# Batched products of x and y: output tiles of four heads, stored in 32 KB runs

## The chip, the core and the metric

The kernel runs on one core of a Trainium2 chip. The metric is the device time of one execution in microseconds (us), and lower is better. The core has five engines: TensorE (PE, matrix products), VectorE (DVE), ScalarE (ACT), GpSimd (POOL) and SyncE (SP, which here issues transfers), and 16 DMA engines that move data between the chip's main memory (HBM) and the on-chip memory (SBUF, 128 partitions). PE writes its products to PSUM, 128 partitions of eight banks of 2 KB. Weight loads of PE have a row of their own, PEld.

## The reference

```
x: (8, 12, 512, 64) float32      y: (8, 12, 512, 64) float32
out = np.einsum('bhtc,bhsc->bhts', x, y)      # (8, 12, 512, 512) float32
```

For each of the 96 heads (8 batches of 12) the output is the 512 x 512 matrix of dot products of the rows of x with the rows of y, over 64 channels. The inputs are 25.17 MB together, the output is 100.66 MB.

## The kernel before

The heads are taken in six groups of 16. One load brings x or y of a group, 2 MB, as 128 partitions of 64 rows of 64 channels (16 KB each), so that eight partitions hold a head. There are 12 loads, x and y in turn, numbered n = 0 to 11.

Each group is worked on in two halves of eight heads (turns; 12 in all). Several steps turn a loaded tile into operands of PE:

- `compress(n)`: x is cast to bf16 by ACT into `xk`. y is cast in four pieces of 64 partitions into `yb`, two for each half; DVE makes two, POOL and ACT one each (`in_front`).
- `mix(i, name, part)`: four copies of 32 partitions place x of half i in `xb`, in every second bf16 word; the other words stay zero from a memset, so that a product over 128 rows picks out one of two heads' rows. POOL makes these copies for halves 0 to 2, DVE for the rest.
- `transposes(i)`: DVE transposes `xb` into `xT` and `yb` into `yT`, in 32 x 32 blocks. There are two each of `xb`, `xT` and `yT`, one for each parity of the turn.
- `products()`: PE's whole program, a loop with waits. For each of four values of h (a pair of heads) it multiplies eight times 128 columns of `xT` with 512 of `yT`. Four matmuls fill a PSUM tile `pm` of four banks; there are two such tiles, and together they are all of PSUM. PE waits on the semaphore `turned` for a turn's operands and on `taken` for a free `pm`.
- `result(o, s)`: ACT copies the two `pm` tiles of output tile o into the slot s (L251), and `store` sends the slot out. An output tile is 128 partitions of 8 rows of 512 floats: 16 KB in each partition, and 16 KB in one run in HBM.

Loads and output tiles share five slots of 16 KB per partition, dealt out in turn by `slot()`. Each slot has a semaphore of its own for its transfers. Stores are issued by SP, but by ACT for every third tile and the last four:

```
    def by_act(o):
        return o % 3 == 2 or o >= V * NH - V
```

The order on each engine is the order of the Python program; `emit` works out the waits from what each step reads and writes. The last block lays the front out by hand: five loads, two memsets, then for each n the cast, one mixing copy on POOL, the next load, and from n = 8 on the first results among the casts. After it, each turn i is four results, then `prepare(i + 2)`: the transposes for turn i + 2 and DVE's four mixing copies for turn i + 3.

Of the kernel before, what the change touches and what calls it, by code (L numbers as in the profile page):

```python
# [10 lines left out]
def kernel(  # L11
# [25 lines left out]
    P = 128  # L37
# [6 lines left out]
    K = 8  # L44
    E = R // K
    D = 32
    SLOTS = 5
# [9 lines left out]
        "(o u h q n) -> o h q u n", u=2, h=V, q=Q * E, n=K * S  # L57
# [7 lines left out]
    xbs = [sb.tile([P, K * E * D], u32, name=f"xb{half}") for half in range(2)]  # L65
    xTs = [sb.tile([P, K * D * E], u32, name=f"xT{i}") for i in range(2)]
    yTs = [sb.tile([P, D * R // 2], u32, name=f"yT{i}") for i in range(2)]
# [10 lines left out]
    def need(name, points):  # L78

        best = {}  # L80
        for p, v in points:
            if known[name].get(p, 0) < v:
                best[p] = max(best.get(p, 0), v)
        for p, v in list(best.items()):
            if any(snaps[q, w].get(p, 0) >= v for q, w in best.items() if q != p):
                del best[p]
        if name == "pe":
            asked.append(best)
        for p, v in best.items():
            if name != "pe":  # L90
                engines[name].wait_ge(sems[p], v)  # L91
            known[name][p] = v
            for q, w in snaps[p, v].items():
                known[name][q] = max(known[name].get(q, 0), w)

    def emit(name, make, reads=(), writes=(), dma=None, tells=None):

        points = [writer[r] for r in (*reads, *writes) if r in writer]
        points += [v for w in writes for v in readers.get(w, ())]
        if name == "pool" and name in ticks:  # L100
            points.append((name, ticks[name]))
        need(name, points)
        p, step = (tells or name, 1) if dma is None else (f"dma{dma}", 16)
        sem(p)
        at = (p, ticks.get(p, 0) + step)
        ticks[p] = at[1]
        snaps[at] = {**known[name], p: at[1]}
        if dma is None:
            own[name][p] = at[1]
            snaps[at].update(own[name])  # L110
        if name != "pe":
            make().then_inc(sems[p], step)
        for r in reads:
            readers.setdefault(r, []).append(at)
        for w in writes:
            writer[w], readers[w] = at, []

    made_slots, loaded, later, asked = [], {}, [], []
    in_front = ["dve", "pool", "dve", "act"]

    def copy(name, dst, src, reads, writes, tells=None):
        emit(
            name,
            lambda: nc.scalar.activation(dst, src, COPY)  # L124
            if name == "act"
            else engines[name].tensor_copy(dst, src),  # L126
            reads,
            writes,
            tells=tells,
        )  # L130

    def both(i):
        return [("slot", i, 0), ("slot", i, 1)]

    def slot():
        made_slots.append(len(made_slots) % SLOTS)
        return made_slots[-1]

    def load(n):
        i = loaded[n] = slot()  # L140
        emit(
            "sp",
            lambda: nc.sync.dma_start(slots[i], (yv if n % 2 else xv)[n // 2]),  # L143
            writes=both(i),
            dma=i,
        )

    def compress(n):

        i = loaded.pop(n)  # L150
        g = n // 2
        if n % 2 == 0:
            xk = g % (NG - 1)
            dst = xks[xk].rearrange("p r c -> p (r c)")
            copy("act", dst, slots[i], both(i), [("xk", xk)])
            return
        ys = slots[i].rearrange("p (r c) -> p r c", c=C)
        for half in range(2):
            b = g % (NG - 1 + half)
            yv2 = ybs[half][b].bitcast(bf16).rearrange("p (j c w) -> p j w c", j=R // 2, w=2)  # L160
            for ch in range(2):
                copy(
                    in_front[2 * half + ch],
                    yv2[ch * 64:(ch + 1) * 64],
                    ys[half * 64:(half + 1) * 64, :, ch * D:(ch + 1) * D].rearrange(
                        "p (j w) c -> p j w c", w=2
                    ),
                    both(i),
                    [("yb", half, b, ch)],
                )  # L170

    def mix(i, name, part):
# [5 lines left out]
        xv2 = xbs[half].bitcast(bf16).rearrange("p (k e c u) -> p k e c u", k=K, e=E, u=2)  # L178
        copy(
            name,  # L180
            xv2[part * D:(part + 1) * D, :, :, :, u],
            xks[xk][lo:lo + D, :, ch * D:(ch + 1) * D].rearrange("p (e k) c -> p k e c", k=K),
            [("xk", xk)],
            [("xb", half, part)],
        )

    def transposes(i):
        g, half = divmod(i, 2)
        b = g % (NG - 1 + half)
        emit(  # L190
            "dve",
            lambda: nc.vector.transpose(  # L192
                xTs[half].rearrange("p (k r e) -> p k e r", k=K, e=E),
                xbs[half].rearrange("p (k e c) -> p k e c", k=K, e=E),
            ),
            [("xb", half, part) for part in range(4)],
            [("xT", half)],
        )
        emit(
            "dve",  # L200
            lambda: nc.vector.transpose(  # L201
                yTs[half].rearrange("p (r j) -> p j r", r=D),
# [3 lines left out]
            [("yT", half)],  # L206
            tells="turned",
        )

    def products():  # L210

        pe = mybir.EngineType.PE
        with nc.Fori(0, NH // 2, engines=OrderedEngineSet([pe])) as turn:
            for half in range(2):
                xT = xTs[half].bitcast(bf16).rearrange("p (k h m) -> p k h m", k=K, h=V)
                yT = yTs[half].bitcast(bf16)
                nc.tensor.wait_ge(sem("turned"), turn * 2 + (half + 1))
                for h in range(V):
                    for k in range(0, K, 4):
                        done = 2 * (half * V + h) + k // 4  # L220
                        nc.tensor.wait_ge(sem("taken"), turn * (4 * V) + (done + 1))
                        for j in range(4):
                            last = nc.tensor.matmul(  # L223
                                pms[k // 4][:, j, :], xT[:, k + j, h, :], yT[:, h * S:(h + 1) * S],
                                start=True, stop=True,
                            )
                        last.then_inc(sem("pe"), 1)

    def by_act(o):
        return o % 3 == 2 or o >= V * NH - V  # L230

    def store(o, s):
        i, h = divmod(o, V)
        name = "act" if by_act(o) else "sp"
        emit(
            name,
            lambda: engines[name].dma_start(ov[i, h], slots[s]),
            reads=both(s),
            dma=s,
        )  # L240

    def result(o, s):

        ot = slots[s].rearrange("p (r s) -> p r s", s=S)
        for k in range(0, K, 4):
            pm = k // 4
            half = o // V % 2
            emit("pe", None, [("xT", half), ("yT", half)], [("pm", pm)])
            want = {"turned": o // V + 1, "taken": 2 * o + pm + 1}
            assert all(want.get(p, 0) >= v for p, v in asked[-1].items()), (o, k, asked[-1])  # L250
            copy("act", ot[:, k:k + 4, :], pms[pm], [("pm", pm)], [("slot", s, pm)], "taken")  # L251
            if k == 0:
                while later:
                    store(*later.pop())
        if by_act(o):
            later.append((o, s))
        else:
            store(o, s)

    def prepare(i):  # L260

        if i < NH:
            transposes(i)
        if i + 1 < NH:
            for part in range(4):
                mix(i + 1, "dve", part)

    with tc.tile_critical():  # L268
        nc.scalar.sem_inc(sem("taken"), 2)
        ticks["taken"] = 2  # L270
        for g in range(SLOTS):
            load(g)
        for half, name in enumerate(("dve", "pool")):
            emit(
                name,
                lambda: engines[name].memset(xbs[half], 0.0),  # L276
                writes=[("xb", half, part) for part in range(4)],
            )
        front = []
        for n in range(2 * NG):  # L280
            if n == 11:
                result(3, slot())
            compress(n)
            mix(n // 4, "pool", n % 4)
            if n == 4:
                transposes(0)
            if n < 5:
                load(n + SLOTS)
            elif n in (6, 8):
                load(n // 2 + 7)  # L290
            elif n < 10:
                front.append(slot())
            if n > 7 and n < 11:
                result(n - 8, front[n - 8])
            if n == 9:
                transposes(1)
        prepare(2)
        for o in range(V, V * NH):
            result(o, slot())
            if o % V == V - 1:  # L300
                prepare(o // V + 2)
        store(*later.pop())
        products()
        for i, name in enumerate(("dve", "pool", "dve", "sp", "act")):
            need(name, [(f"dma{i}", ticks[f"dma{i}"])])
# [30 lines left out]
```

## Time and profile before

| | |
|---|---|
| median of 3 runs | 301.12 us (301.08 to 301.19) |
| the profiled execution: its time, its span | 301.19 us, 299.4 us |
| ACT busy | 211.0 us (70%) |
| DVE busy | 151.8 us (51%) |
| PE busy, mean granted clock | 127.1 us (42%), 0.834 |
| POOL busy | 56.1 us (19%) |
| DMA moved | 125.85 MB, mean 420 GB/s |
| stores issued by SP, by ACT | 30, 18 (2 MB each) |
| loads issued by SP | 12 (2 MB each) |

The span runs from the first to the last instruction of the profiled execution; its time also holds what lies around that. Busy times overlap, since the engines run side by side. A group of instructions is named by line, engine, operation and tiles, output first (`slot<-pm` is a copy out of PSUM). Idle time is put down to what ended it.

### The profile page before, as it was taken

What the parts mean: (1) busy time and instruction counts of PE and PEld (TensorE: products, weight loads), DVE (VectorE), ACT (ScalarE), POOL (GpSimd) and SP (SyncE); (2) the same over time, 40 slices, a digit from 0 to 9 for tenths busy, and PEclk for the clock granted to TensorE, in tenths of its full rate; (3) what the DMA queues carried; (4) which work ended last, traced back from release to release, by engine and by line L of the source; (5) the groups of instructions that cost most, each with busy time, mean ns of one, the idle gap of its engine ahead of it and who ended that gap; (6) DMA issues with size and microseconds to landing.
All of it is one profiled execution on the core that took longest, in us unless ns stands there. A gap on an engine that the chain in (4) does not pass through costs nothing.

```text
span 299.4 us, 1276 instructions
## 1 busy us (share of the span) xinstructions
PE 127.1 (42%) x378; PEld 34.5 (12%) x384; DVE 151.8 (51%) x73; ACT 211.0 (70%) x109; POOL 56.1 (19%) x23
## 2 busy tenths in 40 slices
PE   0000040546566554565544556454646454736000
PEld 0000010111111111111111111111111111111000
DVE  2167897999839592920946729219276340000000
ACT  1665676999999886767686868585959595959400
POOL 2399999991000000000000000000000000000000
PEclk9999999958799979695979595979595979596855
DMA  7999999999999999999999999999999999999995
GB/s 276 423 433 433 427 423 431 431 429 425 427 438 427 431 436 428 429 433 431 429 433 430 425 429 440 425 427 433 427 429 425 425 429 427 429 427 425 429 427 234
DMA packets 8643, 125.85 MB, mean 420 GB/s; under 512 B 961, under 2 KB 961, under 8 KB 961
## 3 DMA queue, kind: packets, MB, share of 16 engines
q1 hardware_dynamic: 6048, 88.08, 69.3%
q10 hardware_dynamic: 2592, 37.75, 29.6%
q14 instruction: 3, 0.02, 0.0%
HBM read 25.17 MB, written 100.66 MB: 420 GB/s over the span
## 4 chain that ended last, share of the span: by engine, by line
DMA 57%; ACT 22%; PE 6%; issue 6%; DVE 2%; SPq 0%; ACTq 0%
DMA out_dram<-slot 44%; ACT slot L124 20%; DMA slot<-in_y_dram 7%; DMA slot<-in_x_dram 6%; PE pm L223 6%; DVE yb L126 2%; ACT xk L124 1%; ACT yb L124 1%; SPq L143 0%; ACTq L91 0%; SPq L331 0%; SPq L268 0%
## 5 line engine op out<-in xcount | busy, mean ns | idle before, releaser
L124 ACT ACTIVATE slot<-pm 128x2048 f32<-128x2048 f32 x96 | 173.4, 1885 | 46.6 <-DMA out_dram<-slot 43.5
L223 PE MATMUL pm<-yT,xT 128*128 128x512 bf16 x378 | 127.1, 473 | 150.5 <-ACT slot L124 112.5
L192 DVE STREAM_TRANSPOSE xT<-xb 128x2048 uint32<-128x2048 uint32 x12 | 46.6, 3885 | 71.4 <-PE pm L223 69.0
L223 PEld LDWEIGHTS pm<-yT,xT 128*128 128x128 bf16 x384 | 34.5, 111 | 242.6 <-ACT slot L124 170.5
L126 DVE COPY xb<-xk 32x2048 bf16<-32x2048 bf16 x36 | 46.9, 1303 | 1.0
L126 DVE CAST yb<-slot 64x2048 bf16<-64x2048 f32 x12 | 36.2, 3019 | 17.0 <-DMA slot<-in_y_dram 16.8
L126 POOL COPY xb<-xk 32x2048 bf16<-32x2048 bf16 x12 | 36.3, 3022 | 10.5 <-ACT xk L124 9.7
L124 ACT ACTIVATE xk<-slot 128x4096 bf16<-128x4096 f32 x6 | 21.7, 3617 | 16.3 <-DMA slot<-in_x_dram 16.3
L201 DVE STREAM_TRANSPOSE yT<-yb 128x1024 uint32<-128x1024 uint32 x12 | 23.1, 1923 | 0.0
L124 ACT ACTIVATE yb<-slot 64x2048 bf16<-64x2048 f32 x6 | 14.8, 2464 | 5.1 <-DMA slot<-in_y_dram 5.1
L126 POOL CAST yb<-slot 64x2048 bf16<-64x2048 f32 x6 | 17.8, 2968 | 1.4 <-DMA slot<-in_y_dram 0.8
L276 DVE MEMSET xb<- 128x2048 uint32 x1 | 1.8, 1765 | 1.4 <-SPq L268 1.4
L124 ACT ACT_TABLE_LOAD x1 | 1.3, 1283 | 1.0 <-SPq L268 1.0
L276 POOL MEMSET xb<- 128x2048 uint32 x1 | 1.8, 1804 | 0.5 <-SPq L268 0.5
L320 POOL MEMSET const-float32-0.0<- 128x1 f32 x1 | 0.1, 97 | 0.2 <-issue 0.2
L320 POOL MEMSET const-float32-1.0<- 128x1 f32 x1 | 0.1, 98 | 0.0
L320 POOL MEMSET const-bfloat16-1.0<- 128x1 bf16 x1 | 0.1, 98 | 0.0
L320 POOL MEMSET const-uint8-127<- 128x1 uint8 x1 | 0.1, 98 | 0.0
## 6 DMA issues: line engine op xcount, KB each, us to landing
out_dram<-slot SPq DMA_DIRECT2D x30, 2048.0 KB, 16.6
out_dram<-slot ACTq DMA_DIRECT2D x18, 2048.0 KB, 14.7
slot<-in_x_dram SPq DMA_DIRECT2D x6, 2048.0 KB, 17.6
slot<-in_y_dram SPq DMA_DIRECT2D x6, 2048.0 KB, 20.8
```

The costliest lines, as they stand in the source:

```text
L124: lambda: nc.scalar.activation(dst, src, COPY)
L126: else engines[name].tensor_copy(dst, src),
L192: lambda: nc.vector.transpose(xTs[half].rearrange("p (k r e) -> p k e r", k=K, e=E), xbs[half].rearrange("p (k e c) -> p k e c", k=K, e=E),),
L201: lambda: nc.vector.transpose(yTs[half].rearrange("p (r j) -> p j r", r=D), ybs[half][b].rearrange("p (j c) -> p j c", c=D),),
L223: last = nc.tensor.matmul(pms[k // 4][:, j, :], xT[:, k + j, h, :], yT[:, h * S:(h + 1) * S], start=True, stop=True,)
L276: lambda: engines[name].memset(xbs[half], 0.0),
L320: nc = _bacc.Bacc("TRN2", target_bir_lowering=False, num_devices=1)
```

## The change

- K, the rows of an output tile in one partition, goes from 8 to 16, and the 64 rows of an input partition are split as 4 x 16 (E = 4). An output tile o now covers four heads: 128 partitions of 32 KB, 4 MB, and there are 24. Each partition's 32 KB are one run in HBM. All stores are issued by SP.
- There are three slots of 32 KB per partition instead of five of 16 KB. A load takes half a slot (`space`), which gives six load places, each with a semaphore of its own; stores have one for each slot. Load n + 6 goes to the place of load n.
- A matmul has 64 columns of `xT` instead of 128, and its product goes to 64 partitions of a bank. Two of them, one for each of two heads and placed at columns 0 and 64 (`tile_position`), fill a bank. A unit of work is four banks with eight matmuls, and ACT copies it as before, 128 x 2048. There are 96 units as before, eight in a turn.
- There is one `xb`, one `yT`, and one pair of `xT` that holds the two halves of K of one turn. `transposes(i)` is now three steps of 1024 words per partition: the first half of x, y, the second half of x. PE waits for two of them before a turn's first unit and for the third before its third.
- The front: six loads, one memset on POOL, then for n = 0 to 5 load n + 6 behind the casts of n. POOL mixes halves 0 and 1 only, and takes two casts of y for n = 9 and 11 and all of x for n = 10, where ACT did them. DVE mixes from half 2 on. The first units come among the casts from n = 7 on.
- PE itself adds the two free `pm` to `taken`, and the final waits for the last three stores stand on PE, SP and ACT.

The diff, cut to what acts:

```diff
     NG = B * H // G
     NH = 2 * NG
     V = G // 4
-    K = 8
+    K = 16
     E = R // K
     D = 32
-    SLOTS = 5
+    U = K // 4
+    SLOTS = 3
...
     ov = out.rearrange("b h t s -> (b h t s)").rearrange(
-        "(o u h q n) -> o h q u n", u=2, h=V, q=Q * E, n=K * S
+        "(o u t q n) -> o t q u n", u=2, t=2, q=2 * Q * E, n=K * S
     )
 
...
-    xbs = [sb.tile([P, K * E * D], u32, name=f"xb{half}") for half in range(2)]
-    xTs = [sb.tile([P, K * D * E], u32, name=f"xT{i}") for i in range(2)]
-    yTs = [sb.tile([P, D * R // 2], u32, name=f"yT{i}") for i in range(2)]
+    xb = sb.tile([P, R * D], u32, name="xb")
+    xTs = [sb.tile([P, K // 2 * D * E], u32, name=f"xT{i}") for i in range(2)]
+    yT = sb.tile([P, D * R // 2], u32, name="yT")
...
+    def caster(n, half, ch):
+        if n % 2 == 0:
+            return "pool" if n == 10 else "act"
+        return ("dve", "pool", "dve", "pool" if n > 8 else "act")[2 * half + ch]
+
...
+    def space(n):
+        i, j = divmod(n % (2 * SLOTS), 2)
+        return slots[i][:, j * (K * S // 2):(j + 1) * (K * S // 2)], [("slot", i, 2 * j), ("slot", i, 2 * j + 1)]
 
     def load(n):
-        i = loaded[n] = slot()
+        to, where = space(n)
         emit(
             "sp",
-            lambda: nc.sync.dma_start(slots[i], (yv if n % 2 else xv)[n // 2]),
-            writes=both(i),
-            dma=i,
+            lambda: nc.sync.dma_start(to, (yv if n % 2 else xv)[n // 2]),
+            writes=where,
+            dma=f"in{n % (2 * SLOTS)}",
         )
 
...
     def transposes(i):
         g, half = divmod(i, 2)
         b = g % (NG - 1 + half)
+        xe = xb.rearrange("p (e k c) -> p e k c", e=E, c=D)
+
+        def of_x(kh):
+            emit(
+                "dve",
+                lambda: nc.vector.transpose(
+                    xTs[kh].rearrange("p (k r e) -> p e k r", r=D, e=E),
+                    xe[:, :, kh * (K // 2):(kh + 1) * (K // 2), :],
+                ),
+                [("xb", part) for part in range(4)],
+                [("xT", kh)],
+                tells="turned",
+            )
+
+        of_x(0)
         emit(
             "dve",
             lambda: nc.vector.transpose(
-                xTs[half].rearrange("p (k r e) -> p k e r", k=K, e=E),
-                xbs[half].rearrange("p (k e c) -> p k e c", k=K, e=E),
-            ),
-            [("xb", half, part) for part in range(4)],
-            [("xT", half)],
-        )
-        emit(
-            "dve",
-            lambda: nc.vector.transpose(
-                yTs[half].rearrange("p (r j) -> p j r", r=D),
+                yT.rearrange("p (r j) -> p j r", r=D),
                 ybs[half][b].rearrange("p (j c) -> p j c", c=D),
             ),
             [("yb", half, b, ch) for ch in range(2)],
-            [("yT", half)],
+            ["yT"],
             tells="turned",
         )
+        of_x(1)
 
     def products():
 
         pe = mybir.EngineType.PE
-        with nc.Fori(0, NH // 2, engines=OrderedEngineSet([pe])) as turn:
-            for half in range(2):
-                xT = xTs[half].bitcast(bf16).rearrange("p (k h m) -> p k h m", k=K, h=V)
-                yT = yTs[half].bitcast(bf16)
-                nc.tensor.wait_ge(sem("turned"), turn * 2 + (half + 1))
-                for h in range(V):
-                    for k in range(0, K, 4):
-                        done = 2 * (half * V + h) + k // 4
-                        nc.tensor.wait_ge(sem("taken"), turn * (4 * V) + (done + 1))
-                        for j in range(4):
+        xcs = [t.bitcast(bf16).rearrange("p (k h m) -> p k h m", k=K // 2, h=V) for t in xTs]
+        yc = yT.bitcast(bf16)
+        nc.tensor.sem_inc(sem("taken"), 2)
+        with nc.Fori(0, NH, engines=OrderedEngineSet([pe])) as turn:
+            for t in range(2):
+                for v in range(U):
+                    done = t * U + v
+                    if done in (0, U // 2):
+                        nc.tensor.wait_ge(sem("turned"), turn * 3 + (2 + (done > 0)))
+                    nc.tensor.wait_ge(sem("taken"), turn * (2 * U) + (done + 1))
+                    for j in range(4):
+                        kh, k = divmod(4 * v + j, K // 2)
+                        for hs in range(2):
+                            h = 2 * t + hs
                             last = nc.tensor.matmul(
-                                pms[k // 4][:, j, :], xT[:, k + j, h, :], yT[:, h * S:(h + 1) * S],
-                                start=True, stop=True,
+                                pms[v % 2][hs * 64:(hs + 1) * 64, j, :], xcs[kh][:, k, h, :], yc[:, h * S:(h + 1) * S],
+                                start=True, stop=True, tile_position=(0, hs * 64),
                             )
-                        last.then_inc(sem("pe"), 1)
-
-    def by_act(o):
-        return o % 3 == 2 or o >= V * NH - V
-
-    def store(o, s):
-        i, h = divmod(o, V)
-        name = "act" if by_act(o) else "sp"
-        emit(
-            name,
-            lambda: engines[name].dma_start(ov[i, h], slots[s]),
-            reads=both(s),
-            dma=s,
-        )
-
-    def result(o, s):
-
-        ot = slots[s].rearrange("p (r s) -> p r s", s=S)
-        for k in range(0, K, 4):
-            pm = k // 4
-            half = o // V % 2
-            emit("pe", None, [("xT", half), ("yT", half)], [("pm", pm)])
-            want = {"turned": o // V + 1, "taken": 2 * o + pm + 1}
-            assert all(want.get(p, 0) >= v for p, v in asked[-1].items()), (o, k, asked[-1])
-            copy("act", ot[:, k:k + 4, :], pms[pm], [("pm", pm)], [("slot", s, pm)], "taken")
-            if k == 0:
-                while later:
-                    store(*later.pop())
-        if by_act(o):
-            later.append((o, s))
-        else:
-            store(o, s)
-
-    def prepare(i):
-
-        if i < NH:
-            transposes(i)
-        if i + 1 < NH:
-            for part in range(4):
-                mix(i + 1, "dve", part)
+                    last.then_inc(sem("pe"), 1)
+
+    def unit(o, v):
+
+        i = o // 2
+        pm = v % 2
+        emit("pe", None, [("xT", v // 2), "yT"], [("pm", pm)], virtual=True)
+        want = {"turned": 3 * i + (2 if o % 2 == 0 and v < 2 else 3), "taken": o * U + v + 1}
+        assert all(want.get(p, 0) >= w for p, w in asked[-1].items()), (o, v, asked[-1])
+        s = o % SLOTS
+        rows = slots[s].rearrange("p (r s) -> p r s", s=S)[:, 4 * v:4 * v + 4, :]
+        copy("act", rows, pms[pm], [("pm", pm)], [("slot", s, v)], "taken")
+        if v == U - 1:
+            emit(
+                "sp",
+                lambda: nc.sync.dma_start(ov[i, o % 2], slots[s]),
+                reads=[("slot", s, w) for w in range(U)],
+                dma=f"out{s}",
+            )
 
     with tc.tile_critical():
-        nc.scalar.sem_inc(sem("taken"), 2)
+        sem("taken")
         ticks["taken"] = 2
-        for g in range(SLOTS):
-            load(g)
-        for half, name in enumerate(("dve", "pool")):
-            emit(
-                name,
-                lambda: engines[name].memset(xbs[half], 0.0),
-                writes=[("xb", half, part) for part in range(4)],
-            )
-        front = []
+        for n in range(2 * SLOTS):
+            load(n)
+        emit("pool", lambda: nc.gpsimd.memset(xb, 0.0), writes=[("xb", part) for part in range(4)])
         for n in range(2 * NG):
-            if n == 11:
-                result(3, slot())
             compress(n)
-            mix(n // 4, "pool", n % 4)
-            if n == 4:
+            if n < 2 * SLOTS:
+                load(n + 2 * SLOTS)
+            if n < 8:
+                mix(n // 4, "pool", n % 4)
+            if n == 3:
                 transposes(0)
-            if n < 5:
-                load(n + SLOTS)
-            elif n in (6, 8):
-                load(n // 2 + 7)
-            elif n < 10:
-                front.append(slot())
-            if n > 7 and n < 11:
-                result(n - 8, front[n - 8])
-            if n == 9:
+            if 6 < n < 11:
+                for v in (0, 1) if n % 2 else (2, 3):
+                    unit((n - 7) // 2, v)
+            if n == 10:
                 transposes(1)
-        prepare(2)
-        for o in range(V, V * NH):
-            result(o, slot())
-            if o % V == V - 1:
-                prepare(o // V + 2)
-        store(*later.pop())
+        for part in range(4):
+            mix(2, "dve", part)
+        for i in range(1, NH):
+            for o in (2 * i, 2 * i + 1):
+                for v in range(U):
+                    unit(o, v)
+            if i + 1 < NH:
+                transposes(i + 1)
+            if i + 2 < NH:
+                for part in range(4):
+                    mix(i + 2, "dve", part)
         products()
-        for i, name in enumerate(("dve", "pool", "dve", "sp", "act")):
-            need(name, [(f"dma{i}", ticks[f"dma{i}"])])
+        for name, o in (("pe", 2 * NH - 3), ("sp", 2 * NH - 2), ("act", 2 * NH - 1)):
+            need(name, [(f"out{o % SLOTS}", ticks[f"out{o % SLOTS}"])])
```

More of the change, by code (lines that the diff above doesn't have):

```diff
@@ L76, in sem, with need @@
         return sems[p]
-    def need(name, points):
+    def need(name, points, virtual=False):
         best = {}
@@ L86, in need @@
                 del best[p]
-        if name == "pe":
+        if virtual:
             asked.append(best)
         for p, v in best.items():
-            if name != "pe":
+            if not virtual:
                 engines[name].wait_ge(sems[p], v)
@@ L94, in need, with emit @@
                 known[name][q] = max(known[name].get(q, 0), w)
-    def emit(name, make, reads=(), writes=(), dma=None, tells=None):
+    def emit(name, make, reads=(), writes=(), dma=None, tells=None, virtual=False):
         points = [writer[r] for r in (*reads, *writes) if r in writer]
@@ L101, in emit @@
             points.append((name, ticks[name]))
-        need(name, points)
-        p, step = (tells or name, 1) if dma is None else (f"dma{dma}", 16)
+        need(name, points, virtual)
+        p, step = (tells or name, 1) if dma is None else (dma, 16)
         sem(p)
@@ L110, in emit @@
             snaps[at].update(own[name])
-        if name != "pe":
+        if not virtual:
             make().then_inc(sems[p], step)
@@ L116, in emit, with copy @@
             writer[w], readers[w] = at, []
-    made_slots, loaded, later, asked = [], {}, [], []
-    in_front = ["dve", "pool", "dve", "act"]
-    def copy(name, dst, src, reads, writes, tells=None):
+    asked = []
+    def caster(n, half, ch):
+        if n % 2 == 0:
+            return "pool" if n == 10 else "act"
+        return ("dve", "pool", "dve", "pool" if n > 8 else "act")[2 * half + ch]
+    def copy(name, dst, src, reads, writes, tells=None, virtual=False):
         emit(
@@ L129, in copy @@
             tells=tells,
+            virtual=virtual,
         )
[L132 to L137, printed above, removed]
+    def space(n):
+        i, j = divmod(n % (2 * SLOTS), 2)
+        return slots[i][:, j * (K * S // 2):(j + 1) * (K * S // 2)], [("slot", i, 2 * j), ("slot", i, 2 * j + 1)]
     def load(n):
-        i = loaded[n] = slot()
+        to, where = space(n)
         emit(
             "sp",
-            lambda: nc.sync.dma_start(slots[i], (yv if n % 2 else xv)[n // 2]),
-            writes=both(i),
-            dma=i,
+            lambda: nc.sync.dma_start(to, (yv if n % 2 else xv)[n // 2]),
+            writes=where,
+            dma=f"in{n % (2 * SLOTS)}",
         )
     def compress(n):
-        i = loaded.pop(n)
         g = n // 2
+        held, where = space(n)
         if n % 2 == 0:
@@ L154, in compress @@
             dst = xks[xk].rearrange("p r c -> p (r c)")
-            copy("act", dst, slots[i], both(i), [("xk", xk)])
+            copy(caster(n, 0, 0), dst, held, where, [("xk", xk)])
             return
-        ys = slots[i].rearrange("p (r c) -> p r c", c=C)
+        ys = held.rearrange("p (r c) -> p r c", c=C)
         for half in range(2):
@@ L162, in compress @@
                 copy(
-                    in_front[2 * half + ch],
+                    caster(n, half, ch),
                     yv2[ch * 64:(ch + 1) * 64],
@@ L167, in compress @@
                     ),
-                    both(i),
+                    where,
                     [("yb", half, b, ch)],
@@ L177, in mix @@
         xk = g % (NG - 1)
-        xv2 = xbs[half].bitcast(bf16).rearrange("p (k e c u) -> p k e c u", k=K, e=E, u=2)
         copy(
             name,
-            xv2[part * D:(part + 1) * D, :, :, :, u],
-            xks[xk][lo:lo + D, :, ch * D:(ch + 1) * D].rearrange("p (e k) c -> p k e c", k=K),
+            xb[part * D:(part + 1) * D].bitcast(bf16).rearrange("p (r c u) -> p r c u", c=D, u=2)[:, :, :, u],
+            xks[xk][lo:lo + D, :, ch * D:(ch + 1) * D],
             [("xk", xk)],
-            [("xb", half, part)],
+            [("xb", part)],
         )
```

## The prediction

> **What bounds the kernel now.** I read the page's DMA rows first, since 125.85 MB must move whatever the engines do. DMA is the mean busy share of 16 DMA engines, in tenths, over 40 slices of the span.
>
> ```profile
> PE 127.1 (42%) x378; PEld 34.5 (12%) x384; DVE 151.8 (51%) x73; ACT 211.0 (70%) x109; POOL 56.1 (19%) x23
> ...
> DMA  7999999999999999999999999999999999999995
> GB/s 276 423 433 433 427 423 431 431 429 425 427 438 427 431 436 428 429 433 431 429 433 430 425 429 440 425 427 433 427 429 425 425 429 427 429 427 425 429 427 234
> DMA packets 8643, 125.85 MB, mean 420 GB/s; under 512 B 961, under 2 KB 961, under 8 KB 961
> ```
>
> Only the first and the last slice are not full, and no engine is above 70%. The timeline (start, duration, engine, work, idle before it) shows loads landing back to back, since each of these waits ends on a landing:
>
> ```profile
> 8.79 3.62 ACT L124 ACTIVATE xk<-slot 128x4096 bf16<-128x4096 f32 x1 [6.54 <-DMA slot<-in_x_dram]
> ...
> 13.66 2.44 ACT L124 ACTIVATE yb<-slot 64x2048 bf16<-64x2048 f32 x1 [1.25 <-DMA slot<-in_y_dram]
> ...
> 18.56 3.62 ACT L124 ACTIVATE xk<-slot 128x4096 bf16<-128x4096 f32 x1 [2.46 <-DMA slot<-in_x_dram]
> ```
>
> One 2 MB transfer takes 4.88 us. Twelve loads and 48 stores are 60 x 4.88 = 292.8 us; 3.9 before the first and 2.7 after the last make the 299.4 span. The profiled execution took 301.19, 1.79 beyond its span; the runs' median is 301.12, 0.07 away. So two things can move the time: the rate of the queue, and a moment at which it runs dry. What could dry it is in the groups (busy us, mean ns of one, idle before and its releaser) and in the timeline of PE:
>
> ```profile
> L124 ACT ACTIVATE slot<-pm 128x2048 f32<-128x2048 f32 x96 | 173.4, 1885 | 46.6 <-DMA out_dram<-slot 43.5
> ...
> L223 PEld LDWEIGHTS pm<-yT,xT 128*128 128x128 bf16 x384 | 34.5, 111 | 242.6 <-ACT slot L124 170.5
> L126 DVE COPY xb<-xk 32x2048 bf16<-32x2048 bf16 x36 | 46.9, 1303 | 1.0
> ...
> L126 POOL COPY xb<-xk 32x2048 bf16<-32x2048 bf16 x12 | 36.3, 3022 | 10.5 <-ACT xk L124 9.7
> ...
> L201 DVE STREAM_TRANSPOSE yT<-yb 128x1024 uint32<-128x1024 uint32 x12 | 23.1, 1923 | 0.0
> ...
> L126 POOL CAST yb<-slot 64x2048 bf16<-64x2048 f32 x6 | 17.8, 2968 | 1.4 <-DMA slot<-in_y_dram 0.8
> ```
> ```profile
> 176.84 1.04 PE L223 MATMUL pm<-yT,xT 128*128 128x512 bf16 x4 [0.73 <-ACT slot L124]
> ...
> 182.34 3.66 PE L223 MATMUL pm<-yT,xT 128*128 128x512 bf16 x8 [4.46 <-ACT slot L124]
> ```
>
> ACT's copies idle 43.5 us for stores to land: the engines are ahead of the queue. Four matmuls take 1.04 us at the full granted clock and half of 3.66, 1.83 us, after a pause.
>
> **Stores of 32 KB runs.** The 24 stores of 4 MB replace 48 of 2 MB: the same bytes, half as many runs. In the trace's packet records a 16 KB run takes a median 611 ns of its DMA engine, and the only other size, two 8 KB instruction fetches during the run, 309. A line through both is 302 ns per 8 KB and 7 ns fixed, so 32 KB should take 1215 instead of 1222. Each engine moves 24 x 8 = 192 such runs: 192 x 7 = 1.3 us. Each store ends with a 9 ns semaphore packet per engine; 24 fewer are 0.2 us. Sum: -1.5 us, all on the path. Bounds: the best 16 KB packet took 608 ns, the mean 615, so 384 packets at the best are -2.8; stores after 200 us ran at 616, and all 384 at that instead of the mean 614 of the store phase are +0.8. No gain at all if runs are cut at 16 KB, the largest packet shown. I take -1.5, the line through the two sizes.
>
> The Trainium skill (DMA: Bandwidth & Descriptors, Anatomy of one DMA) fits a fixed 2.0 us per DMA plus bytes over 436 GB/s; 24 fewer DMAs would then save 48 us. The trace speaks against charging that here: 4.88 us from landing to landing is 0.07 above 2 MB at the page's 436 GB/s, so back-to-back transfers hide the fixed part.
>
> All stores now go out by SP; before, 18 went by ACT. One queue alone held 430 GB/s from 10 to 50 us, as fast as two later, so this costs nothing. SP has two 0.54 us issues per turn of 8 units, far apart.
>
> **Columns in halves.** A unit (4 PSUM banks, one 1.885 us copy) was 4 matmuls and is now 8 of 64 columns, two per bank. The trace has no such matmul. If the two halves run side by side, a unit stays at 1.04 to 1.83 us; if one after the other, at 2.08 to 3.66. I take side by side: the nearest row fills the same 128 columns from the same 128 rows. A unit may take up to 2.2 us before it matters (below).
>
> The skill speaks against it (TensorEngine Tiling (Array Packing), Gotcha 2): column tiling excludes Fast Weight Load. By the trace a weight load is 111 ns and lies beside running matmuls; eight laid bare would be 0.9 us per unit, 1.9 us at the full clock, still under the limit, and 2.7 on the slow one, over it.
>
> **One set of transposed inputs.** yT and the second half of xT of turn i+1 wait until PE has done turn i. Then DVE turns yT (1.92), PE fills a unit (1.83) while ACT still copies the last one (1.885): ACT idles some 1.9 us once per turn. A turn is 8 x 1.885 + 1.9 = 17.0 us of ACT; its two stores take 2 x 9.77 = 19.5. DVE spends 3 x 1.92 + 4 x 1.30 = 11.0 per turn. Both stay under the queue: zero, with 2.5 us per turn of cover. If PE sets the pace instead, 8 units + 2 us pass 19.5 when a unit passes 2.2.
>
> **Three slots.** A slot lands, is filled in 7.5 us (9.5 across a turn), is issued, and its first packet follows about 1.0 us later (load 0: issued at 0.96, first packet at 1.98). The other two slots cover 2 x 9.77 = 19.5 us. Zero; 9 us of cover.
>
> **The front.** Six loads start at once instead of five; the seventh is issued when ACT has cast x0 (12.4) and the twelfth after y2's casts (about 44), before its turn at 57.7. Loads end at 62.6 as now. With one xb, POOL's mixing of part 4 waits until DVE has transposed all of half 0: the fourth part is ready at 31.3 as now, three transposes end at 37.1. From there POOL has 4 mixes, 6 casts of y and all of x5 (two casts' worth, 5.9): 4 x 3.02 + 6 x 2.97 + 5.9 = 35.8, done at 72.9. DVE, with casts of 3.4 us beside POOL and transposes of half 1 until 67, ends y5 at about 74. ACT: x3 to 41.8, y3 to 45.5, two units to 49.3, x4 to 52.9, two more to 56.7, where store 0 is issued, 6 us before the loads end. Stores 0 and 1 keep the queue busy to 82.1. Store 2 needs y5's place: 74 + 2 x 1.885 = 77.8, and it must be issued 1.5 us before 82.1, so by 80.6. Zero, with 2.8 us of cover, the thinnest here. With POOL at its slowest rows (3.45, 3.54, 7.1) it ends at 79.2 and store 2 is 2.4 us late. Later stores gain 2.5 us per turn.
>
> **Sum.** 301.2 - 1.5 = 299.7 us, span 297.9. The old tail stays, as the last store still ends in a landing.
>
> **Rivals.** (1) The long run is no cheaper (cut at 16 KB, or at the late rows' rate): 301.0, from 300.9 to 302.0. For it: nothing above 16 KB is shown. Against: the 8 and 16 KB rows. (2) Store 2 late, by up to 2.4 us: 299.7 to 302.1, with no gain on the runs up to 303.5; it decides once y5's place is free later than 76.8. For it: POOL takes on x5 and idles to 37.1. Against: its mean rows. (3) Slower: on PE, the halves of a bank follow one another. It decides at 2.2 us per unit. At the mean clock of 0.81 the x4 row becomes 2 x 1.04 / 0.81 = 2.57, a turn 22.5, 3.0 more than the queue needs, over 11 turns +33: 333 us. For it: the row's pauses and the 1.83 us. Against: at the full clock 2.08 fits, and the granted clock was 1.00 from 90 to 100 us, when units came every 1.77 us.
>
> **How the numbers follow.** What a measurement of this kernel can tell from no change is about 0.2%, 0.6 us. My forecast, 0.56: faster. Rival 1, 0.16 (0.14 same, 0.02 slower); rival 2, 0.15 (faster 0.02, same 0.04, slower 0.09); rival 3, 0.13 (slower). So faster 0.58, same 0.18, slower 0.24. The range runs from 298.4 (every packet at the best, -2.8) to 303.0, near the end of rival 2; rival 3 and little else is left out.
>
> **What would show it.** Right: half the store packets, at 1212 to 1216 ns; ACT's group still idle on out_dram; two-store spacing of 19.4; DMA full in every inner slice; PE units under 2.2 us. Wrong: 16 KB packets or 32 KB ones over 1222 (run step); a gap near 82 us with ACT waiting on POOL or DVE yb (front step); ACT's idle put to PE (columns).

## The result, and the profile after

The changed kernel takes 301.83 us (median of 15 runs, 301.65 to 301.98), the kernel before 301.22 (median of 15, 301.08 to 301.72): 1.0018 times as long, 95% interval 1.0010 to 1.0026. The forecast was 299.7. The profiled execution took 301.98, its span is 300.2.

The page after, its first rows and the DMA rows:

```profile
span 300.2 us, 2037 instructions
...
PE 141.6 (47%) x768; PEld 47.1 (16%) x768; DVE 156.3 (52%) x88; ACT 203.6 (68%) x106; POOL 55.8 (19%) x22
...
DMA  7999999999999999999999999999999999999991
GB/s 271 428 434 432 426 428 428 430 426 450 450 424 419 419 454 450 424 419 420 450 442 428 424 419 445 445 428 428 419 450 441 428 424 419 450 441 428 424 424 83
DMA packets 5186, 125.85 MB, mean 419 GB/s; under 512 B 576, under 2 KB 576, under 8 KB 576
```

The queue is full in every inner slice, as before, and from 60 to 280 us it moves 433 to 434 GB/s where it moved 427 to 432. But the last slice holds 83 GB/s instead of 234, and the kernel is not shorter. The number of instructions, 2037, stands beside 1276 before. The groups:

```profile
L129 ACT ACTIVATE slot<-pm 128x2048 f32<-128x2048 f32 x96 | 174.4, 1879 | 54.1 <-DMA out_dram<-slot 42.7
L236 PE MATMUL pm<-yT,xT 128*64 128x512 bf16 x768 | 141.6, 520 | 133.7 <-ACT slot L129 77.4
L236 PEld LDWEIGHTS pm<-yT,xT 128*64 128x64 bf16 x768 | 47.1, 138 | 227.6 <-ACT slot L129 145.2
```

ACT still waits for stores to land, 42.7 us in all (43.5 before), so the engines are still ahead of the queue. What differs is how the queue ends. Here are stretches of the end (PE, PEld, DVE, ACT, POOL busy, clock, DMA share, GB/s; a packet counts where it starts). First the kernel before:

```profile
295.00:296.00 1.00, 0.00 (x0) 0.00 (x0) 0.00 (x0) 0.00 (x0) 0.00 (x0) 0.50 0.92 393
296.00:297.00 1.00, 0.00 (x0) 0.00 (x0) 0.00 (x0) 0.00 (x0) 0.00 (x0) 0.50 0.05 16
297.00:298.00 1.00, 0.00 (x0) 0.00 (x0) 0.00 (x0) 0.00 (x0) 0.00 (x0) 0.50 0.04 16
```

The changed kernel:

```profile
290.00:294.00 4.00, 0.00 (x0) 0.00 (x0) 0.00 (x0) 0.00 (x0) 0.00 (x0) 0.50 0.93 401
294.00:295.00 1.00, 0.00 (x0) 0.00 (x0) 0.00 (x0) 0.00 (x0) 0.00 (x0) 0.50 0.08 33
295.00:296.00 1.00, 0.00 (x0) 0.00 (x0) 0.00 (x0) 0.00 (x0) 0.00 (x0) 0.50 0.00 0
296.00:297.00 1.00, 0.00 (x0) 0.00 (x0) 0.00 (x0) 0.00 (x0) 0.00 (x0) 0.50 0.08 33
297.00:298.00 1.00, 0.00 (x0) 0.00 (x0) 0.00 (x0) 0.00 (x0) 0.00 (x0) 0.50 0.08 33
```

And the DMA view of the changed kernel from 294.8 to 298.6 us:

```profile
DMA packets 4, 0.10 MB, mean 26 GB/s; under 512 B 1, under 2 KB 1, under 8 KB 1
...
q1 hardware_dynamic: 4, 0.10, 6.0%
```

6.0% of 16 engines is about one engine (1/16 is 6.25%): it sends three more 32 KB packets and a semaphore packet while the other 15 are done. Each store raises its semaphore by 16 increments, one for each DMA engine. In the trace's completion records, 15 of the last store's 16 increments are in by 294.99 us and the last comes at 299.04; before, 296.81 and 298.23. So 15 DMA engines end 1.8 us earlier (1.5 was forecast), one ends 0.8 us later, and the kernel ends with that one. In the packet records its trail is plain: from 66 us on, nearly every 1.24 us one packet takes mostly 5 to 60 ns over the 1213 of all the others, except for a packet or two once per turn of 19.7 us, when PE pauses.

### The profile page after: what moved, and what is told of

It is laid out like the page before. It is cut to its first block, busy times and chain, and to the rows that moved or that the text cites. A ratio compares the mean times of both kernels' runs of the same rounds, so it can differ in the third digit from the quotient of the medians.

```text
span 300.2 us, 2037 instructions
## 1 busy us (share of the span) xinstructions
PE 141.6 (47%) x768; PEld 47.1 (16%) x768; DVE 156.3 (52%) x88; ACT 203.6 (68%) x106; POOL 55.8 (19%) x22
## 4 chain that ended last, share of the span: by engine, by line
DMA 46%; ACT 19%; POOL 18%; PE 5%; DVE 3%; issue 1%; ACTq 0%; POOLq 0%; SPq 0%
DMA out_dram<-slot 44%; ACT slot L129 18%; POOL xb L131 8%; POOL yb L131 8%; PE pm L236 5%; DMA slot<-in_x_dram 3%; DVE xT L197 1%; DVE yT L209 1%; ACT xk L129 1%; POOL xk L131 1%; ACTq L92 0%; POOLq L92 0%; SPq L318 0%; SPq L260 0%
## 5 line engine op out<-in xcount | busy, mean ns | idle before, releaser
L129 ACT ACTIVATE slot<-pm 128x2048 f32<-128x2048 f32 x96 | 174.4, 1879 | 54.1 <-DMA out_dram<-slot 42.7
L236 PE MATMUL pm<-yT,xT 128*64 128x512 bf16 x768 | 141.6, 520 | 133.7 <-ACT slot L129 77.4
L236 PEld LDWEIGHTS pm<-yT,xT 128*64 128x64 bf16 x768 | 47.1, 138 | 227.6 <-ACT slot L129 145.2
L197 DVE STREAM_TRANSPOSE xT<-xb 128x1024 uint32<-128x1024 uint32 x24 | 48.2, 2009 | 36.0 <-PE pm L236 33.6
L131 DVE COPY xb<-xk 32x2048 bf16<-32x2048 bf16 x40 | 55.5, 1387 | 1.3
L131 DVE CAST yb<-slot 64x2048 bf16<-64x2048 f32 x12 | 31.7, 2645 | 23.8 <-DMA slot<-in_y_dram 23.6
L131 POOL COPY xb<-xk 32x2048 bf16<-32x2048 bf16 x8 | 25.3, 3162 | 15.7 <-ACT xk L129 9.7
L129 ACT ACTIVATE xk<-slot 128x4096 bf16<-128x4096 f32 x5 | 18.1, 3617 | 13.8 <-DMA slot<-in_x_dram 13.8
L131 POOL CAST yb<-slot 64x2048 bf16<-64x2048 f32 x8 | 24.9, 3118 | 0.9
L129 ACT ACTIVATE yb<-slot 64x2048 bf16<-64x2048 f32 x4 | 9.8, 2460 | 5.1 <-DMA slot<-in_y_dram 5.1
L131 POOL CAST xk<-slot 128x4096 bf16<-128x4096 f32 x1 | 3.6, 3595 | 0.1
```

Of the source, the lines that this page charges most:

```text
L197: lambda: nc.vector.transpose(xTs[kh].rearrange("p (k r e) -> p e k r", r=D, e=E), xe[:, :, kh * (K // 2):(kh + 1) * (K // 2), :],),
L236: last = nc.tensor.matmul(pms[v % 2][hs * 64:(hs + 1) * 64, j, :], xcs[kh][:, k, h, :], yc[:, h * S:(h + 1) * S], start=True, stop=True, t ...
```

## The experiments

Theory A: one DMA engine loses a few ns for each matmul with its weight load; 384 more of both cost it more than the longer runs save. (Experiment 5 asks whether instructions of another engine count too.) Rivals: B, the long runs or large slots make one engine late; C, the single queue does it. What is called the tail is the stretch at the end in which one DMA engine alone is still at work.

**1. The kernel before, matmuls in halves** (A against B and C).

```diff
-                            last = nc.tensor.matmul(
-                                pms[k // 4][:, j, :], xT[:, k + j, h, :], yT[:, h * S:(h + 1) * S],
-                                start=True, stop=True,
-                            )
+                            for cs in range(0, P, 64):
+                                last = nc.tensor.matmul(
+                                    pms[k // 4][cs:cs + 64, j, :], xT[:, k + j, h, cs:cs + 64],
+                                    yT[:, h * S:(h + 1) * S],
+                                    start=True, stop=True, tile_position=(0, cs),
+                                )
```

> The kernel before, with each 128-column matmul made as two of 64 columns (768 matmuls instead of 378 recorded); stores stay at 16 KB runs, five slots, two queues. Theory A (one of the 16 DMA engines loses about 6 to 7 ns per matmul with its weight load, and the store that ends last waits for it): that engine loses some 2.5 us more, 301.2 becomes 302.8 to 303.8. Theory B (the longer runs or the bigger slots make one engine late): no change, 301.2. Theory C (the stores' single queue does it): no change, 301.2.

Measured: 302.97 us, ratio 1.0056 (1.0042 to 1.0070). Nothing of the stores was touched, and the end grows a tail like that of the changed kernel:

```profile
295.00:296.00 1.00, 0.00 (x0) 0.00 (x0) 0.00 (x0) 0.00 (x0) 0.00 (x0) 0.50 0.96 410
296.00:297.00 1.00, 0.00 (x0) 0.00 (x0) 0.00 (x0) 0.00 (x0) 0.00 (x0) 0.50 0.09 33
297.00:298.00 1.00, 0.00 (x0) 0.00 (x0) 0.00 (x0) 0.00 (x0) 0.00 (x0) 0.50 0.08 33
298.00:299.00 1.00, 0.00 (x0) 0.00 (x0) 0.00 (x0) 0.00 (x0) 0.00 (x0) 0.50 0.08 33
```

Fifteen increments are in by 297.11 (296.81 before), the last at 299.98 (298.23). That is inside A's range and against B and C. The kernel before took 301.31 us in this round of runs (301.21 in that of experiments 5 to 9), so times of different rounds compare to about 0.1 us.

**2. The changed kernel with wide matmuls.**

```diff
-        xcs = [t.bitcast(bf16).rearrange("p (k h m) -> p k h m", k=K // 2, h=V) for t in xTs]
+        xws = [t.bitcast(bf16).rearrange("p (k t m) -> p k t m", k=K // 2, t=2) for t in xTs]
...
-                        for hs in range(2):
-                            h = 2 * t + hs
-                            last = nc.tensor.matmul(
-                                pms[v % 2][hs * 64:(hs + 1) * 64, j, :], xcs[kh][:, k, h, :], yc[:, h * S:(h + 1) * S],
-                                start=True, stop=True, tile_position=(0, hs * 64),
-                            )
+                        last = nc.tensor.matmul(
+                            pms[v % 2][:, j, :], xws[kh][:, k, t, :], yc[:, 2 * t * S:(2 * t + 1) * S],
+                            start=True, stop=True,
+                        )
```

> The changed kernel with one 128-column matmul per bank instead of two of 64, 384 instead of 768. It leaves out the second head's own y: both heads of a bank are multiplied by the first one's. Stores, slots and front are those of the changed kernel. Theory A (a loss per matmul on one DMA engine): that engine ends 2.0 to 2.8 us earlier, 301.8 becomes 299.0 to 299.8. Theory B (long runs or slots): no change, 301.8. Theory C (single queue): no change, 301.8.

Measured: 300.26 us, ratio to before 0.9970 (0.9960 to 0.9980), 0.5 us above A's range: the 6 to 7 ns per matmul with its weight load was too high a price, and the table below gives 4 to 5. The long runs, slots, front and single set of operands are all there; only the number and width of the matmuls are back, and with them the time goes below the kernel before. The tail shrinks:

```profile
span 298.2 us, 1269 instructions
```
```profile
294.00:295.00 1.00, 0.00 (x0) 0.00 (x0) 0.00 (x0) 0.00 (x0) 0.00 (x0) 0.50 0.08 33
295.00:296.00 1.00, 0.00 (x0) 0.00 (x0) 0.00 (x0) 0.00 (x0) 0.00 (x0) 0.50 0.08 33
296.00:297.00 1.00, 0.00 (x0) 0.00 (x0) 0.00 (x0) 0.00 (x0) 0.00 (x0) 0.50 0.00 0
```

Increments: 15 by 294.95, the last at 297.05.

**3. The changed kernel with two queues** (C).

```diff
+            name = "act" if o % 3 == 2 else "sp"
             emit(
-                "sp",
-                lambda: nc.sync.dma_start(ov[i, o % 2], slots[s]),
+                name,
+                lambda: engines[name].dma_start(ov[i, o % 2], slots[s]),
```

> The changed kernel, with every third store issued by ACT as before. Theory A (a loss per matmul on one DMA engine): no change, 301.8. Theory B (long runs or slots): no change. Theory C (with a single queue one engine falls behind): back to 15 engines and the last one closer together, 299.5 to 300.5.

Measured: 301.95 us, ratio to before 1.0021 (1.0012 to 1.0030). No change from the changed kernel's 301.83 (1.0018); C falls.

**4. The last store in parts**, meant to leave the late engine out at the end. Rows 0 to 7 of each partition go out as 64 x 2 partitions, then rows 8 to 15 as 60 x 2 and 4 x 2.

```diff
+        if o == 2 * NH - 1 and v % 2:
+            c = slice(v // 2 * 4096, v // 2 * 4096 + 4096)
+            for q in (slice(0, 64),) if v == 1 else (slice(0, 60), slice(60, 64)):
+                emit(
+                    "sp",
+                    lambda: nc.sync.dma_start(ov[i, o % 2][q, :, c], slots[s][2 * q.start:2 * q.stop, c]),
...
```

> The changed kernel, with the last 4 MB store cut in two by rows: the first 16 KB of each partition as one transfer over 64 x 2 partitions, the second 16 KB as one of 60 x 2 and one of 4 x 2 partitions. If a transfer of 60 rows uses 15 engines and the late engine is the one left out, it has 8 packets of 16 KB (4.9 us) less to do at the end and four others have two more (1.2 us): 301.8 becomes 299.0 to 299.8. If the late engine is among the 15, the four get later or the late one keeps its time: 301.8 to 303.5. Theory A and B both leave this open; it tells whether the late engine alone sets the end.

Measured: 305.04 us, ratio 1.0125 (1.0110 to 1.0141), outside both expectations. Of the last store's 256 packets of 16 KB, 47 take over 1200 ns, 1268 or 1269 most often, where 163 take 611. So the remedy cost more than the lateness, and the run says nothing on the late engine. Why the packets are slow was not tested.

**5. Other instructions, and 6. other matmuls.** Experiment 5 adds work on POOL that touches no product; experiment 6 doubles the matmuls of the kernel before without half-width products.

```diff
+    spare = sb.tile([P, 1], fp32, name="spare")
...
+        for _ in range(768):
+            emit("pool", lambda: nc.gpsimd.memset(spare, 0.0), writes=[("spare",)])
```

> The kernel before, with 768 memsets of one float per partition on POOL, each waiting for the one before, from about 70 us on, when POOL is otherwise done. Theory A1 (the late DMA engine loses some ns for every instruction of any engine): 768 x 2.3 to 4.6 ns, 301.3 becomes 303.0 to 304.8. Theory A2 (only PE's matmuls cost it time): no change beyond instruction fetches, 301.3 to 301.8.

```diff
+                            for n in range(0, S, S // 2):
+                                last = nc.tensor.matmul(
+                                    pms[k // 4][:, j, n:n + S // 2], xT[:, k + j, h, :],
+                                    yT[:, h * S + n:h * S + n + S // 2],
...
```

> The kernel before, with each matmul of 512 moving columns made as two of 256; all 128 columns of weights, nothing placed in half the array. Theory A (the number of matmuls and weight loads counts): as with the halves of 64 columns, 301.3 becomes 302.6 to 303.3. Theory D (the half-width products or their writes to half the partitions of a bank count): no change, 301.3.

Measured: 304.04 us with the memsets (ratio 1.0096, 1.0080 to 1.0111) and 303.06 with the short matmuls (1.0062, 1.0049 to 1.0076). The tail of the run with memsets (the DMA view from 296.8 to 301 us) is again one engine's, 6.4% of 16:

```profile
DMA packets 9, 0.11 MB, mean 27 GB/s; under 512 B 2, under 2 KB 2, under 8 KB 2
...
q10 hardware_dynamic: 9, 0.11, 6.4%
```

Both times lie in the ranges of theories A1 and A. So it is not the half-width placement (D), and not PE alone (A2): instructions of POOL cost the late engine time too. The memsets bring six more instruction fetches of 8 KB (309 ns each, 1.9 us together). Some at least seem to have fallen on another engine: 14 increments of the last store are in by 296.50, one comes at 298.12, and the last at 301.07. Had all six fallen on the late one, 1.0 of the 2.83 us would still be the memsets'.

**7. PE's loop written out**, in the kernel before.

```diff
-        with nc.Fori(0, NH // 2, engines=OrderedEngineSet([pe])) as turn:
+        for turn in range(NH // 2):
```

> The kernel before, with PE's loop written out, waits on constants: some 130 register instructions and branches of PE fewer, some 40 KB of instructions more to fetch. Theory A1 (every instruction costs): 130 x 2.3 ns or more, 301.3 becomes 300.7 to 301.0, if the fetches (309 ns per 8 KB) fall on other DMA engines than the late one; up to 303 if all fall on it. Theory A2 (matmuls alone): 301.3 but for the fetches.

Measured: 301.18 us, ratio 0.9995 (0.9986 to 1.0004), with 1166 instructions instead of 1276. At 2.35 ns each (below) the 110 instructions fewer should save 0.26 us, and the interval holds both that and nothing: inconclusive.

**8. and 9. Fewer matmuls in both kernels**, as a check that the price also runs downwards. Both have `range(0, 4, 2)` for `range(4)`, after eight matmuls that fill all banks once; experiment 9 builds on experiment 2.

> The kernel before with half of its matmuls: two of four banks of a unit keep the products of the first four (200 matmuls, 200 weight loads; half of the products are left out). All copies and stores stay. Theory A1 (every instruction costs one DMA engine 2.2 ns): 368 instructions fewer are 0.8 us, 301.2 becomes 300.2 to 300.6. Theory E (the cost per matmul sets in only above the count of before, the late engine being late for another reason): no change, 301.2.

> The changed kernel with 128-column matmuls and half of them left out: two of four banks of a unit keep the products of the first four (200 matmuls instead of 768, both heads of a bank against the first one's y). Theory A1: 0.8 us below the version with 384 such matmuls, 300.3 becomes 299.3 to 299.7. Theory E: no change from that version, 300.3.

Measured: 300.31 us (ratio 0.9968, 0.9957 to 0.9978) and 299.15 us (0.9933, 0.9919 to 0.9946). The first is inside A1's range, the second 0.15 us below it; theory E, which has no change in either, falls. The pages' first lines:

```profile
span 298.5 us, 914 instructions
```
```profile
span 297.4 us, 901 instructions
```

All together, median time by instructions on the page:

| runs of | about 900 | about 1270 | about 2040 |
|---|---|---|---|
| 16 KB | 300.31 (914) | 301.22 (1276) | 302.97 (2050), 303.06 (2050) |
| 32 KB | 299.15 (901) | 300.26 (1269) | 301.83 (2037) |

Along the first row, 302.97 - 300.31 = 2.66 us over 1136 instructions is 2.34 ns each; along the second, 2.68 us over 1136 is 2.36. Between neighbouring cells it is 2.0 to 3.0 ns, so the close agreement of the two is in part luck. Between the rows, the long runs with all that came with them save 1.16, 0.96 and 1.14 us. The change is the way from 301.22 to 301.83: about -1.1 for the runs and 761 x 2.35 ns = +1.8 for the instructions, +0.7 in sum where +0.6 was measured.

The packet records give the price without the run times. With 32 KB runs nearly all packets after 66 us take 1213 ns, and the excess of those that take 4 to 129 ns more adds up to 4.44 us in the changed kernel (1776 instructions start after 66 us), 2.86 in experiment 2 (1080) and 1.99 in experiment 9 (732). From first to last, 2.45 us over 1044 instructions is again 2.35 ns each, and at no instructions that line leaves 0.3 us. So the late engine loses its time all along the run, in step with the instructions, and this loss is not a fixed cost of the end.

## Why the prediction was wrong

The step that failed is the sentence that closes the sum, "the old tail stays", together with **columns in halves**, which costed 384 more matmuls at nothing as long as a unit stayed under 2.2 us. Their cover, PE's spare time, was real; but they cost in a place that the sum did not have, one DMA engine's time, which is on the path: about +1.8 us where the sum had nothing, against about -1.1 from the runs where it had -1.5. The trace of before showed that place: one engine ended at 297.75 us in its packet records while 15 were done by 296.6. I read the 2.7 us after the last transfer as a fixed tail and not as an engine that had lost time throughout, and did not ask what lengthens it. The last store landed at 298.23 of a span of 299.4, so only 1.1 of these 2.7 us came after the last landing; the rest was the late engine.

The stated range, 298.4 to 303.0, holds the measured time by luck: its upper part was made for rivals 1 and 2, and neither happened.

**Stores of 32 KB runs**: right in mechanism, mis-sized. A 32 KB packet takes 1213 ns (1215 by the line through 8 and 16 KB, and 1212 to 1216 was named). Fifteen engines gained 1.8 us, more than the 1.5, perhaps since the slower packets late in the run are gone too: after 200 us the median was 615 ns for 16 KB before and is 1213 for 32 KB now. The whole time gained less: about 1.1 us by the table. The spacing of two stores should have been 19.4 us and was 19.8 (landings at 72.19, 91.95, 111.81), since a store lands when its late engine has; that sign was named, though not tied to any step. The fit of 2.0 us per DMA that was set aside there (the Trainium skill, DMA: Bandwidth & Descriptors, Anatomy of one DMA) is the page's for transfers issued by GpSimd, and here GpSimd issues none.

**The other side of columns in halves**: right. The timeline of PE, a unit of eight matmuls at the full clock and two after a pause:

```profile
88.14 1.05 PE L236 MATMUL pm<-yT,xT 128*64 128x512 bf16 x8 [0.53 <-ACT slot L129]
...
103.88 3.69 PE L236 MATMUL pm<-yT,xT 128*64 128x512 bf16 x16 [0.75 <-ACT slot L129]
```

1.05 us for eight against 1.04 for four: the halves run side by side, and rival 3 falls. The page of the Trainium skill that was weighed there (TensorEngine Tiling (Array Packing), Gotcha 2) says that column tiling excludes Fast Weight Load. A weight load took 138 ns instead of 111 with half the columns, and there are twice as many, but a unit's length shows none of it. My sum had no cost outside PE.

**The front, three slots, one set of operands**: right. POOL and ACT around the third store:

```profile
62.84 3.60 POOL L131 CAST xk<-slot 128x4096 bf16<-128x4096 f32 x1
66.56 6.82 POOL L131 CAST yb<-slot 64x2048 bf16<-64x2048 f32 x2
```
```profile
73.50 3.65 ACT L129 ACTIVATE slot<-pm 128x2048 f32<-128x2048 f32 x2 [3.28 <-POOL yb L131]
```

POOL is done at 73.4 (forecast 72.9), x5 cheaper than the two casts taken for it (3.6, not 5.9) and y5 dearer. Store 0 was issued at 57.0 (56.7); the copies for store 2 end at 77.2 (77.8), with the queue busy until 82. Rival 2 had its wait, 3.28 us of ACT, and its cover held. The wait forecast for the one set of operands, 1.9 us of ACT per turn, was mostly hidden: ACT waited 5.3 us for PE in the whole run.

**Rival 1** (a long run is no cheaper) gave 300.9 to 302.0 and holds the measured time, for a wrong reason: the runs are cheaper, and experiment 2 shows it. A tail that grows with the instructions was not among the rivals.

No version here that computes the whole output is clearly faster than the kernel before. In this layout a partition with 16 rows of a head leaves a product 64 columns of one pair of heads, so runs of 32 KB come with the 768 matmuls; other layouts were not tried.

## What to carry to other kernels

When a kernel is bound by its transfers, look at the slowest DMA engine and not at the mean: a store ends with its last engine, and a last stretch with 6% of the engines busy is one of them. Before changing how many instructions a unit takes, price them there too; in these kernels 100 instructions more cost about 0.23 us, though the engine that ran them had time to spare. Half as many runs, with the larger stores and slots that go with them, was worth 1.1 us; twice as many matmuls cost 1.8. All times here come from runs with recording on, and whether the price stands without it was not shown.

## What the runs showed of the hardware

In these kernels, which keep the DMA engines full, one of the 16 loses about 2.3 ns for each matmul or weight load (2.0 to 3.0 between neighbouring cells of the table). For each POOL memset with its wait it loses up to 3.7 ns (2.83 us over 768), less if some of the new instruction fetches fell on it. What takes the time on that engine is open: each timed run here has a recorded span and clock, so it may be the records of the instructions rather than the instructions, and no run left them out. The Trainium skill (DMA: Bandwidth & Descriptors, Latency and other measured facts) says that two of the engines are usually slower in traces and gives the descriptor rings of transfers issued by GpSimd as a best guess; here GpSimd issues none, one engine is late all the same, and by an amount that follows the instructions. The kept trace does not number the engines, so no run here shows whether it is one of those two.

A 32 KB packet took 1213 ns of its engine, a 16 KB packet 611 and an 8 KB instruction fetch during the run 309. Where the last store went as transfers of 64 x 2, 60 x 2 and 4 x 2 partitions (experiment 4), 47 of its 256 packets of 16 KB took over 1200 ns.
